# Norm gains in the splits of the transposed tiles, another order of the first loads, and part of the high parts on POOL

## The chip, the core and the metric

The kernel runs on one core of a Trainium2 chip. The core has five engines that run side by side, each through its own list of instructions in order: TensorE (PE in the profile; PEld is its loading of weights), VectorE (DVE), ScalarE (ACT), GpSimd (POOL), and SyncE (SP), which here issues nearly all DMA transfers. They wait for each other by semaphores. Matmuls read SBUF and write PSUM. The metric is the device time of one execution in microseconds (us), the median of several.

## What is computed

Two layers of an encoder on 512 tokens of width 1024. Each layer has a mixer (12 token heads of self-attention in 3 key/value groups, and 4 heads of attention to a memory of 256 rows) and a gated feed-forward block, each with a norm before and after it. What matters here is how the norms before the products go into them:

```python
def rms_norm(x, g):
    xf = x.astype(jnp.float32)
    y = xf * lax.rsqrt(jnp.mean(xf * xf, axis=-1, keepdims=True) + EPS)
    return (y * g.astype(jnp.float32)).astype(x.dtype)
...
    mem_n = rms_norm(mem, mem_norm_g)
    for i in range(DEPTH):
        h = rms_norm(x, g_mix_pre[i])
        proj = h @ w_in[i]                  # queries, keys, values, memory queries
        ...
        mkv = mem_n @ w_mem_kv[i]           # memory keys and values
```

The gain g scales the 1024 columns of x or mem, and so the rows of the weight that multiplies them: it may be applied to either side of the product. The row factor (rsqrt) is applied to the product's rows, behind the matmul.

## The kernel before

**Products in three parts.** Products run in fp32r, a format that keeps part of fp32. Each fp32 operand is split into a high part (hi, a copy rounded to fp32r) and a low part (lo = operand - hi), and each product is three matmuls: hi by hi, hi by lo, lo by hi (`mm3`, L275 to L279). `split` (L281) makes the two parts: hi on ACT or, with bit 2 of its argument set, on POOL; lo on DVE or, with bit 1 set, on POOL. `split_scaled` (L298) does the same and multiplies by a factor of one value per partition; its lo is always DVE's.

**Layer 0's mixer.** x and mem come already transposed from HBM (`xT`, `memT`: 128 channels by 8 chunks by 128 tokens). `start` (L1152) issues the first loads and splits token tile 0 into hT (hi and lo), then the key/value weights `wkv` in four units of 768 columns, with token tile 1 after the second unit; `parts(t)` splits a token tile in two instructions of 128x512 per part, `mem_parts(m)` a memory tile in one of 128x1024. Token tiles 2 and 3, memory tiles 0 and 1 and the row factors of x (`factors`: two sums of squares on ACT, then three small operations on POOL, and a fourth for the queries) come later, at due times in the table `LATE`.

Then PE computes keys and values for four token tiles from hT and `wkv` (24 matmuls a tile, in pieces of two channel chunks; tiles 0 and 1 interleaved), the first half of the memory keys and values from mT and `wm` units 0 and 1 (24 matmuls), query group 0 from hT and `wq`, and with it the second half of the memory product, then the other query groups among the heads. `again` (L416) copies the keys' high part on POOL into a third section that the transposes at L430 read. `normalise` (L616) scales the softmax rows p on POOL before they are transposed at L636.

**Weights.** `unit` (L212) loads a weight unit into one of three raw buffers (`raw`, L265) and splits it into one of four pairs whi and wlo. In layer 0 it gets the norm's gain as `g`: where `side` is even it uses `split_scaled`; where it is odd (lo on POOL) it first scales the raw weight in place on POOL (L243) and then splits it. The sides stand in the table `PACE`: for layer 0, `wkv` 0, 0, 2, 0; `wm` 2, 1, 1, 0; `wq` 1, 0, 0, 1 for groups 0 and 1, and 3 for all units of groups 2 and 3.

**What sets the order.** PE's order is the program's order, which `mixer` (L676) writes by sorting pieces by due time. On the other engines the scheduler orders instructions by readiness and program order when the program is built; once built, each engine runs its list in order. The first loads are chained on SP (`queued`, L1200), each after the one before; `self.after` (L188, L223) keeps the first weights of `unit` behind the memory's loads.

Of the kernel before, what the change touches and what calls it, by code (L numbers as in the profile page):

```python
# [16 lines left out]
P = 128  # L17
# [168 lines left out]
class Trunk:  # L186
    def __init__(self, tc, a):
        self.tc, self.nc, self.a, self.nraw, self.more, self.after = tc, tc.nc, a, 0, None, None  # L188
        self.pairs, self.todo, self.stores = {}, [], []
# [22 lines left out]
    def unit(self, src, side=0, pool=None, parts=1, put=None, x=0, dst=None, key=None, g=None, raw=None, pair=None):  # L212
# [3 lines left out]
        own = raw  # L216
# [9 lines left out]
        def load():  # L226
            raw = own or self.raw()
            hi, lo = [(pool or self.whl).tile([P, 1024], F32R, tag=z, name=f"w{z}", bufs=4) for z in ("hi", "lo")]
            if not own:
                with self.tc.issue_after(self.after) if self.after else nullcontext():  # L230
                    nc.sync.dma_start(raw[:, :n], src)
            return raw, hi, lo
# [150 lines left out]
    def mem_pieces(self, l, mk, put, x0, dx, lag, xw):  # L383
# [3 lines left out]
        for u in range(4):  # L387
            self.unit(self.a["wm"][l, u], self.side(l, "mw", u), put=put, x=xw[u], dst=w, key=u,
                      g=self.gcol[:, 1, 2 * u:2 * u + 2])
# [119 lines left out]
    def q_pieces(self, l, c, qTs, put, x0, lead):  # L509
        nc = self.nc  # L510
        w = {}
        for z in range(2):
            self.unit(self.a["wq"][l, c, z], self.side(l, "qw", 2 * c + z), put=put, x=x0 - lead + z * lead / 3, dst=w,
                      key=z, g=None if l else self.gcol[:, 0, 4 * z:4 * z + 4], pair=("wq", l, c, z))
# [161 lines left out]
    def mixer(self, l, mkp, late, tokp):  # L676
# [53 lines left out]
        if l == 0:  # L730
            put(0, lambda: setattr(self, "after", None))
# [420 lines left out]
    def start(self, mkp):  # L1152
# [3 lines left out]
        with ExitStack() as st:  # L1156
# [24 lines left out]
            def parts(t):  # L1181
                for q in range(2):
                    c = slice(t * P, t * P + P)
                    self.split(self.hT[0][q][:, :, c], self.hT[1][q][:, :, c], xT[t][:, 4 * q:4 * q + 4])

            def mem_parts(m):
                c = slice(m * P, m * P + P)
                self.split(self.mT[:, 0, :, c], self.mT[:, 1, :, c], mT[m])

            parts(0)  # L1190
            self.wkv = []
            for u in range(4):
                self.wkv.append(self.unit(a["wkv"][0, u], side=self.side(0, "kw", u), g=gcol[:, 0, 2 * u:2 * u + 2],
                                          raw=raw[u]))
                if u == 1:
                    parts(1)
# [16 lines left out]

        def loads():
            turn(2)
            row(0)
            row(1)
            turn(3)
            row(2)
            for m in range(2):  # L1220
                mT.append(turned("memT"))
                queued(mT[m], a["memT"][m])
            self.after = last[-1]
            row(3)

# [126 lines left out]
```

## Time and profile before

| | us |
|---|---|
| median of 3 runs (1119.73 to 1121.31) | 1120.67 |
| the profiled execution, whole | 1120.98 |
| its span, first to last instruction | 1119.2 |
| PE busy in the span | 1092.2 |
| DVE busy | 835.4 |
| ACT busy | 660.9 |
| POOL busy | 203.3 |

The profiled execution is 0.3 us above the median; some 1.8 us of it lie outside the span. The views used below are these. The page has busy times, and the costliest groups of instructions: line, engine, operation, tiles as out<-in, shape, count, then busy us, mean ns of one, idle us of the engine before them and what ended it. The waits list who waited for whom: us in total, times, longest. The timeline has start, length, engine, line, operation, tiles, shape, count, and in brackets the idle time before and who ended it. Windows give, for a stretch, its length, the busy us and count of PE, PEld, DVE, ACT and POOL, the granted TensorE clock, the DMA share and GB/s. PE's busy time counts a matmul's whole length, of which neighbours overlap a part.

### The profile page before, as it was taken

To read this page: it belongs to the slowest core of one execution; us is meant where nothing else is said; L and a number is where in the kernel's file an instruction comes from. 1 tells how busy PE (TensorE), PEld (TensorE's weight loads), DVE (VectorE), ACT (ScalarE), POOL (GpSimd) and SP (SyncE) were. 2 spreads that over 40 slices of the span, in tenths; PEclk is the share of its full clock that TensorE was granted. 3 is DMA by queue.
4 is the path that set the end of the run, shared out by engine and by line. 5 is a ranking of instruction groups with operands and counts; after the bars stand their busy time and mean duration, and the time that the engine had idled before them with its cause. 6 is when DMAs were issued, how large, how long until landed. Compare 5 with 4: busy or idle time off the path is not lost.

```text
span 1119.2 us, 19475 instructions
## 1 busy us (share of the span) xinstructions
PE 1092.2 (98%) x7438; PEld 1002.9 (90%) x7438; DVE 835.4 (75%) x1399; ACT 660.9 (59%) x1347; POOL 203.3 (18%) x349
## 2 busy tenths in 40 slices
PE   8989999999999999999999999999999999999997
PEld 6879988899989989998899888878999899899986
DVE  5568886899656867885797988757996478669855
ACT  7568995665435544553566888756665255345631
POOL 3685331201100000000343553312000000000001
PEclk9899999999999999999999999999999999999999
DMA  8521115533752382326453221145136223413253
GB/s 331 213 71 39 39 38 189 189 119 120 254 198 79 111 288 87 97 95 206 147 193 114 76 76 38 39 149 183 47 114 210 73 76 114 150 58 99 89 169 113
DMA packets 40558, 142.43 MB, mean 127 GB/s; under 512 B 4625, under 2 KB 5009, under 8 KB 40337
## 3 DMA queue, kind: packets, MB, share of 16 engines
q1 hardware_dynamic: 40176, 140.66, 37.3%
q8 instruction: 58, 0.95, 0.4%
q10 hardware_dynamic: 288, 0.53, 0.1%
q14 instruction: 36, 0.29, 0.1%
HBM read 122.30 MB, written 18.87 MB: 126 GB/s over the span
## 4 chain that ended last, share of the span: by engine, by line
PE 82%; DVE 5%; POOL 5%; ACT 4%; issue 2%; DMA 2%; DVEq 0%; POOLq 0%; SPq 0%; ACTq 0%
PE ps L278 12%; PE ps L277 12%; PE ps L279 12%; PE ps L1036 12%; PE ps L1034 12%; PE ps L1035 12%; PE tp L636 3%; PE o L651 2%; PE o L650 2%; PE s L575 1%; PE s L576 1%; POOL raw L243 1%; POOL wlo L289 1%; DVE tl L291 1%; POOL r L311 1%
## 5 line engine op out<-in xcount | busy, mean ns | idle before, releaser
L287 ACT ACTIVATE whi<-raw 128x1024 fp32r<-128x1024 f32 (+2 forms) x186 | 158.5, 863 | 178.4 <-PE ps L1036 73.5
L291 DVE TENSOR_TENSOR wlo<-raw,whi 128x1024 fp32r<-128x1024 f32 (+2 forms) x178 | 175.3, 995 | 72.4 <-ACT whi L287 69.7
L1035 PE MATMUL ps<-sf,wlo 128*128 128x256 f32 x640 | 179.7, 281 | 0.0
L1034 PE MATMUL ps<-sf,whi 128*128 128x256 f32 x640 | 179.7, 281 | 0.0
L1036 PE MATMUL ps<-sf,whi 128*128 128x256 f32 x640 | 179.7, 281 | 0.0
L277 PE MATMUL ps<-whi,f 128*128 128x512 f32 (+1 forms) x360 | 138.6, 385 | 0.0
L278 PE MATMUL ps<-wlo,f 128*128 128x512 f32 (+1 forms) x360 | 138.5, 385 | 0.0
L279 PE MATMUL ps<-whi,f 128*128 128x512 f32 (+1 forms) x360 | 138.4, 384 | 0.0
L1036 PE MATMUL ps<-a,whi 128*128 128x256 f32 x480 | 134.4, 280 | 0.0
L1034 PE MATMUL ps<-a,whi 128*128 128x256 f32 x480 | 134.3, 280 | 0.0
L1035 PE MATMUL ps<-a,wlo 128*128 128x256 f32 x480 | 133.8, 279 | 0.0
L1035 PEld LDWEIGHTS ps<-sf,wlo 128*128 128x128 f32 x640 | 121.4, 190 | 0.5
L1034 PEld LDWEIGHTS ps<-sf,whi 128*128 128x128 f32 x640 | 121.1, 189 | 0.5
L1036 PEld LDWEIGHTS ps<-sf,whi 128*128 128x128 f32 x640 | 121.4, 190 | 0.0
L320 POOL TENSOR_SCALAR e<-sso 128x1 f32<-128x1 f32 x8 | 3.4, 420 | 563.8 <-ACT junk L315 563.6
L277 PE MATMUL ps<-whi,hT 128*128 128x256 f32 (+1 forms) x320 | 99.0, 309 | 0.8 <-ACT whi L304 0.8
L278 PE MATMUL ps<-wlo,hT 128*128 128x256 f32 (+1 forms) x320 | 94.4, 295 | 1.8 <-DVE wlo L291 1.3
L626 POOL TENSOR_SCALAR p<-p,rd 128x256 f32<-128x256 f32 (+2 forms) x128 | 76.5, 616 | 101.3 <-DVE rd L623 42.0
L279 PE MATMUL ps<-whi,hT 128*128 128x256 f32 (+1 forms) x320 | 93.9, 293 | 0.0
L1035 PEld LDWEIGHTS ps<-a,wlo 128*128 128x128 f32 x480 | 90.5, 188 | 0.2
L1034 PEld LDWEIGHTS ps<-a,whi 128*128 128x128 f32 x480 | 90.5, 188 | 0.2
L1036 PEld LDWEIGHTS ps<-a,whi 128*128 128x128 f32 x480 | 90.1, 188 | 0.0
(205 smaller groups left out, 2729.5 us busy)
## 6 DMA issues: line engine op xcount, KB each, us to landing
raw<-in_wgu_dram SPq DMA_DIRECT2D x48, 512.0 KB, 4.4
raw<-in_wd_dram SPq DMA_DIRECT2D x44, 512.0 KB, 4.3
rb<-in_wgu_dram SPq DMA_DIRECT2D x40, 512.0 KB, 3.6
raw<-in_wo_dram SPq DMA_DIRECT2D x17, 512.0 KB, 3.6
raw<-in_wq_dram SPq DMA_DIRECT2D x16, 512.0 KB, 5.5
xt<-x SPq DMA_DIRECT2D x12, 512.0 KB, 5.0
raw<-in_wm_dram SPq DMA_DIRECT2D x8, 512.0 KB, 3.7
x<-y SPq DMA_DIRECT2D x8, 512.0 KB, 3.0
```

Of the source, the lines that this page charges most:

```text
L277: mm(out, lh, rh, start=first, stop=False)
L278: mm(out, lh, rl, start=False, stop=False)
L279: mm(out, ll, rh, start=False, stop=last)
L287: a = nc.scalar.activation(hi, src, AF.Copy)
L291: b = nc.vector.tensor_sub(lo, src, hi.bitcast(F32))
L626: self.pooled = nc.gpsimd.tensor_scalar(hd["p"][z][:, :n], hd["p"][z][:, :n], rd[:, z:z + 1], 1.0, op0=OP.mult, op1=OP.mult)
L636: nc.tensor.transpose(tp[:, z], hd["p"][i][:, jj * P:(jj + 1) * P], self.ident)
L650: nc.tensor.matmul(o[:, c0:c1], hd["v"](j), th, start=(j == 0), stop=False, skip_group_check=True)
L651: nc.tensor.matmul(o[:, c0:c1], hd["v"](j), tl, start=False, stop=last, skip_group_check=True)
L1034: mm(out, wh[:, s], rh, start=start and k == 0, stop=False, skip_group_check=True)
L1035: mm(out, wl[:, s], rh, start=False, stop=False, skip_group_check=True)
L1036: mm(out, wh[:, s], rl, start=False, stop=k == 3, skip_group_check=True)
```

## The change

The gain moves from the weights to the other operand. `parts` and `mem_parts` now call `split_scaled` chunk by chunk (128x128, eight for a tile) with the gain of that chunk, and weights are split without a gain. For token tiles 1 to 3 and both memory tiles the high parts of the odd chunks are made on POOL. Since no unit has `g` any more, the in-place scaling on POOL does not occur, and a `wkv` unit is split whole (unit 0 in two halves). Of token tile 0 the first four chunks are split ahead of `wkv` unit 0, the last four behind it, and tile 1 behind unit 1.

The first loads are chained in another order: `wm` unit 0 goes ahead of the second row tile, memory tile 0 behind the last token tile, `wm` unit 1 ahead of memory tile 1, and the first `wq` unit behind the last row tile. They fill three raw buffers early (`early`), and `self.after` is gone.

```diff
-    def unit(self, src, side=0, ..., g=None, raw=None, pair=None):
+    def unit(self, src, side=0, ..., g=None, raw=None, pair=None, early=None):
-        own = raw
+        own = raw or self.early.pop(early, None)
...
-                with self.tc.issue_after(self.after) if self.after else nullcontext():
-                    nc.sync.dma_start(raw[:, :n], src)
+                nc.sync.dma_start(raw[:, :n], src)
...
             self.unit(self.a["wm"][l, u], self.side(l, "mw", u), put=put, x=xw[u], dst=w, key=u,
-                      g=self.gcol[:, 1, 2 * u:2 * u + 2])
+                      early=("wm", u) if l == 0 else None)
...
-                      key=z, g=None if l else self.gcol[:, 0, 4 * z:4 * z + 4], pair=("wq", l, c, z))
+                      key=z, pair=("wq", l, c, z), early=("wq", z) if l == c == 0 else None)
...
-            def parts(t):
-                for q in range(2):
-                    c = slice(t * P, t * P + P)
-                    self.split(self.hT[0][q][:, :, c], self.hT[1][q][:, :, c], xT[t][:, 4 * q:4 * q + 4])
+            def parts(t, qs=range(2)):
+                c = slice(t * P, t * P + P)
+                for k in range(4 * qs[0], 4 * qs[-1] + 4):
+                    self.split_scaled(self.hT[0][k // 4][:, k % 4, c], self.hT[1][k // 4][:, k % 4, c], xT[t][:, k],
+                                      gcol[:, 0, k:k + 1], 2 * (t > 0 and k % 2))
             def mem_parts(m):
                 c = slice(m * P, m * P + P)
-                self.split(self.mT[:, 0, :, c], self.mT[:, 1, :, c], mT[m])
-            parts(0)
+                for k in range(KD):
+                    self.split_scaled(self.mT[:, 0, k, c], self.mT[:, 1, k, c], mT[m][:, k], gcol[:, 1, k:k + 1],
+                                      2 * (k % 2))
+            parts(0, (0,))
             self.wkv = []
             for u in range(4):
-                self.wkv.append(self.unit(a["wkv"][0, u], side=self.side(0, "kw", u), g=gcol[:, 0, 2 * u:2 * u + 2],
-                                          raw=raw[u]))
-                if u == 1:
-                    parts(1)
+                self.wkv.append(self.unit(a["wkv"][0, u], side=self.side(0, "kw", u), raw=raw[u], parts=1 if u else 2))
+                if u < 2:
+                    parts(*((0, (1,)), (1,))[u])
...
         def loads():
             turn(2)
             row(0)
+            raw("wm", 0, a["wm"][0, 0])
             row(1)
             turn(3)
+            mem_turn(0)
             row(2)
-            for m in range(2):
-                mT.append(turned("memT"))
-                queued(mT[m], a["memT"][m])
-            self.after = last[-1]
+            raw("wm", 1, a["wm"][0, 1])
+            mem_turn(1)
             row(3)
+            raw("wq", 0, a["wq"][0, 0, 0])
```

PE's list is the same before and after. Three places on DVE and POOL show how the others moved; each row is a line, an operation, tiles as out<-in, a shape and how often it stands there in a row. The changed kernel's lines are one lower up to L680 or so (L290 is the subtraction of `split`, L304 that of `split_scaled`).

DVE's first instructions, from the first low parts of token tile 0 on, before:

```order
L291 TENSOR_TENSOR hT<-xT,hT 128x4x128 x2
L305 SCALAR_TENSOR_TENSOR wlo<-raw,cst,whi 128x384 x4
L291 TENSOR_TENSOR hT<-xT,hT 128x4x128 x2
L305 SCALAR_TENSOR_TENSOR wlo<-raw,cst,whi 128x384 x4
L291 TENSOR_TENSOR hT<-xT,hT 128x4x128 x2
```

and now:

```order
L304 SCALAR_TENSOR_TENSOR hT<-xT,cst,hT 128x128 x4
L290 TENSOR_TENSOR wlo<-raw,whi 128x384 x2
L304 SCALAR_TENSOR_TENSOR hT<-xT,cst,hT 128x128 x6
L290 TENSOR_TENSOR wlo<-raw,whi 128x768
L304 SCALAR_TENSOR_TENSOR hT<-xT,cst,hT 128x128 x6
L290 TENSOR_TENSOR wlo<-raw,whi 128x768 x2
L304 SCALAR_TENSOR_TENSOR hT<-xT,cst,hT 128x128 x8
```

The low part of `wkv` unit 1 stood right behind that of unit 0; now six parts stand between them, the last two of them of token tile 1 (its chunks 1 and 3, whose high parts are POOL's).

POOL from a row factor of x (e, rs, rs, rq) to the first weights of the memory and query products, before (k are the keys that `again` copies):

```order
L320 TENSOR_SCALAR e<-ss 128x1
L325 TENSOR_TENSOR rs<-e,ss 128x1
L326 TENSOR_TENSOR rs<-rs,mhalf 128x1
L1234 TENSOR_SCALAR rq<-rs 128x1
L302 TENSOR_SCALAR whi<-raw,cst 128x512 x2
L418 TENSOR_SCALAR k_484<-k_484 128x3x64
L243 TENSOR_SCALAR raw<-raw,cst 128x512 x2
L289 TENSOR_TENSOR wlo<-raw,whi 128x512
L243 TENSOR_SCALAR raw<-raw,cst 128x256
L289 TENSOR_TENSOR wlo<-raw,whi 128x512
L243 TENSOR_SCALAR raw<-raw,cst 128x256 x3
L289 TENSOR_TENSOR wlo<-raw,whi 128x512 x2
```

and now:

```order
L284 TENSOR_SCALAR whi<-raw 128x512 x2
L417 TENSOR_SCALAR k_375<-k_375 128x3x64
L301 TENSOR_SCALAR mT<-memT,cst 128x128 x3
L319 TENSOR_SCALAR e<-ss 128x1
L324 TENSOR_TENSOR rs<-e,ss 128x1
L325 TENSOR_TENSOR rs<-rs,mhalf 128x1
L1243 TENSOR_SCALAR rq<-rs 128x1
L288 TENSOR_TENSOR wlo<-raw,whi 128x512 x2
L301 TENSOR_SCALAR mT<-memT,cst 128x128
L417 TENSOR_SCALAR k_445<-k_445 128x3x64
L301 TENSOR_SCALAR mT<-memT,cst 128x128 x3
```

The first memory weight (whi) stood behind the row factor of the last token tile; now it stands two row factors earlier, that of tile 2 behind it and that of tile 3 behind the second memory weight (wlo) and the second memory tile. The row factor of tile 3 and the wlo of the first query weight follow.

POOL around the two copies of the memory keys (k, 128x4x64), before:

```order
L243 TENSOR_SCALAR raw<-raw,cst 128x256 x2
L418 TENSOR_SCALAR k_766<-k_766 128x4x64
L243 TENSOR_SCALAR raw<-raw,cst 128x256 x5
L285 TENSOR_SCALAR whi<-raw 128x512 x2
L418 TENSOR_SCALAR k_791<-k_791 128x4x64
L289 TENSOR_TENSOR wlo<-raw,whi 128x512 x2
L243 TENSOR_SCALAR raw<-raw,cst 128x256 x5
L626 TENSOR_SCALAR p<-p,rd 128x256
```

and now:

```order
L284 TENSOR_SCALAR whi<-raw 128x512 x2
L417 TENSOR_SCALAR k_816<-k_816 128x4x64
L288 TENSOR_TENSOR wlo<-raw,whi 128x512 x2
L284 TENSOR_SCALAR whi<-raw 128x512 x2
L417 TENSOR_SCALAR k_841<-k_841 128x4x64
L288 TENSOR_TENSOR wlo<-raw,whi 128x512 x2
L625 TENSOR_SCALAR p<-p,rd 128x256
```

The scaling of raw weights is gone, and the split of one query unit of group 2 (two wlo and, for the next unit, two whi) has moved between the two copies.

More of the change, by code (lines that the diff above doesn't have):

```diff
@@ L187, in __init__ @@
     def __init__(self, tc, a):
-        self.tc, self.nc, self.a, self.nraw, self.more, self.after = tc, tc.nc, a, 0, None, None
+        self.tc, self.nc, self.a, self.nraw, self.more, self.early = tc, tc.nc, a, 0, None, {}
         self.pairs, self.todo, self.stores = {}, [], []
@@ L210, in ahead, with unit @@
             self.stores = [(self.pairs[(name, *at)][z], pair[z].bitcast(F32)) for z in range(2)]
-    def unit(self, src, side=0, pool=None, parts=1, put=None, x=0, dst=None, key=None, g=None, raw=None, pair=None):
+    def unit(self, src, side=0, pool=None, parts=1, put=None, x=0, dst=None, key=None, g=None, raw=None, pair=None, early=None):
         nc, n = self.nc, src.shape[-1]
-        own = raw
+        own = raw or self.early.pop(early, None)
         if pair in self.pairs:
@@ L730, in mixer @@
         if l == 0:
-            put(0, lambda: setattr(self, "after", None))
             put(-0.5, lambda: nc.gpsimd.tensor_scalar(self.nsink, self.sink, -1.0, 1.0, op0=OP.mult, op1=OP.mult))
@@ L1212, in turn, with mem_turn, raw @@
                 queued(xT[t][:, 4 * z:4 * z + 4], a["xT"][t, z])
+        def mem_turn(m):
+            mT.append(turned("memT"))
+            queued(mT[m], a["memT"][m])
+        def raw(name, u, src):
+            self.early[name, u] = self.raw()
+            queued(self.early[name, u], src)
         def loads():
```

## The prediction

> **What bounds the kernel now.** I read the page's busy times first, then the waits of PE over the first 130 us, then PE's timeline where those waits lie, then windows over the same stretch.
>
> ```profile
> PE 1092.2 (98%) x7438; PEld 1002.9 (90%) x7438; DVE 835.4 (75%) x1399; ACT 660.9 (59%) x1347; POOL 203.3 (18%) x349
> PE ps L277 <- POOL whi L302: 4.0, 1, 4.0
> PE tp L430 <- POOL k L418: 3.0, 2, 2.1
> PE tp L636 <- POOL p L626: 1.6, 2, 1.4
> PE ps L278 <- DVE wlo L305: 1.3, 2, 1.0
> ```
>
> TensorE is busy for 98% of the span, its order of instructions is written by hand, and the change leaves that order alone. So time can come only from PE's gaps and from stretches at a low clock. Of the 27 us without a matmul (1119.2 - 1092.2) these four waits hold 9.9, all before 80 us; the first three are for POOL, an engine with 18% load. The change touches layer 0's mixer only, so the rest of the span should run as before. The first gap:
>
> ```profile
> 24.38 0.34 PE L279 MATMUL ps<-whi,hT 128*128 128x384 f32 x1
> 28.72 0.80 PE L277 MATMUL ps<-whi,mT 128*128 128x512 f32 x1 [4.01 <-POOL whi L302]
> 39.59 0.35 PE L277 MATMUL ps<-whi,hT 128*128 128x256 f32 x1
> ```
>
> The key/value products (hT) end at 24.7; the memory products (mT) start at 28.7; the row at 39.59 stands among the first query products. The later gaps, and POOL beside them:
>
> ```profile
> 65.70 0.54 PE L430 MATMUL tp<-identr,k 128*128 128x128 f32 x4 [0.86 <-POOL k L418]
> 69.67 0.54 PE L430 MATMUL tp<-identr,k 128*128 128x128 f32 x4 [2.11 <-POOL k L418]
> 75.12 0.33 PE L636 MATMUL tp<-cst,p 128*128 128x128 f32 x1 [1.40 <-POOL p L626]
> 75.68 0.43 PE L636 MATMUL tp<-cst,p 128*128 128x128 f32 x1 [0.23 <-POOL p L626]
> 65.62 2.46 POOL L243 TENSOR_SCALAR raw<-raw,cst 128x256 f32<-128x256 f32 x5
> 69.22 0.40 POOL L418 TENSOR_SCALAR k<-k 128x256 fp32r<-128x256 f32 x1
> ```
>
> PE stands still for a copy that takes POOL 0.40 us, because POOL first scales raw weights. Then the clock, in windows of 3.41 us laid from where it fell:
>
> ```profile
> 27.92:31.33 3.41, 1.57 (x3) 0.97 (x4) 3.08 (x7) 0.94 (x3) 2.37 (x5) 0.51 0.03 10
> 31.33:34.74 3.41, 3.41 (x10) 2.63 (x9) 0.21 (x1) 1.26 (x2) 3.33 (x5) 0.50 0.67 237
> 65.46:68.87 3.41, 1.86 (x16) 1.72 (x16) 2.09 (x6) 3.06 (x9) 3.41 (x8) 1.00 0.43 149
> 72.29:75.70 3.41, 1.78 (x12) 1.27 (x12) 2.87 (x11) 2.21 (x6) 3.41 (x8) 1.00 0.47 154
> 75.70:79.11 3.41, 3.41 (x17) 3.41 (x18) 1.01 (x4) 1.59 (x5) 0.94 (x2) 0.51 0.00 0
> ```
>
> After the length come the busy times of PE, PEld, DVE, ACT and POOL, then the granted clock. Behind a window with PE busy 1.78 us the clock was 0.51 for one window; behind one with 1.86 it stayed.
>
> **Part 1: POOL no longer scales raw weights (L243).**
>
> ```profile
> L243 POOL TENSOR_SCALAR raw<-raw,cst 128x256 f32<-128x256 f32 x24 | 11.3, 484 | 7.1 <-DMA raw<-in_wq_dram 7.1
> L243 POOL TENSOR_SCALAR raw<-raw,cst 128x512 f32<-128x512 f32 x4 | 3.4, 860 | 0.1
> L289 POOL TENSOR_TENSOR wlo<-raw,whi 128x512 fp32r<-128x512 f32 x15 | 19.6, 1318 | 0.2
> L285 POOL TENSOR_SCALAR whi<-raw 128x512 fp32r<-128x512 f32 x8 | 5.0, 636 | 0.1
> 56.66 0.40 PE L279 MATMUL ps<-whi,mT 128*128 128x512 f32 x1
> ```
>
> All 28 instructions go, 14.7 us of POOL's time. Between the two memory-key copies (k, x4) stand now two whi and two wlo: 2 x 0.64 + 2 x 1.32 = 3.9 us. The product that the first copy needs ends at 57.0 on PE; with 1.5 for its two parts on ACT and DVE the copy ends near 59, the second near 63.5. Without the waits PE wants the second at 69.67 - 2.11 - 0.86 = 66.7. The two wlo behind it end near 66.2, before the first p, which PE wants at 75.12 - 1.40 - 2.97 = 70.8. So all four waits go: 0.86 + 2.11 + 1.40 + 0.23 = 4.6 us. The window at 0.51 goes with them: it lost between nothing and 3.41 x 0.49 = 1.7; I take 1.5, since nearly all of it was matmuls. **Part 1: -6.1 us.** Late next is p's chain on DVE and ACT (minimum, exp, reciprocal), by my sum about 1 us ahead of PE.
>
> **Part 2: the start.**
>
> ```profile
> 4.40 0.31 ACT L1197 ACTIVATE identr<-cst 128x128 fp32r<-128x128 f32 x1 [1.47 <-DMA cst<-in_cst_dram]
> 4.62 0.61 ACT L287 ACTIVATE hT<-xT 128x512 fp32r<-128x512 f32 x1
> 38.90 1.70 ACT L304 ACTIVATE whi<-raw,cst 128x256 fp32r<-128x256 f32 x4
> 52.41 1.67 DVE L305 SCALAR_TENSOR_TENSOR wlo<-raw,cst,whi 128x256 fp32r<-128x256 f32 x4 [0.68 <-ACT whi L304]
> L291 DVE TENSOR_TENSOR hT<-xT,hT 128x512 fp32r<-128x512 f32 x8 | 5.2, 687 | 4.2 <-ACT hT L287 4.1
> 18.10 0.19 POOL L1234 TENSOR_SCALAR rq<-rs 128x1 f32<-128x1 f32 x1
> 8.31 0.34 PE L277 MATMUL ps<-whi,hT 128*128 128x384 f32 x1
> 20.29 0.41 PE L277 MATMUL ps<-whi,hT 128*128 128x384 f32 x1
> ```
>
> A split of 128x512 becomes four scaled ones of 128x128, a form that the trace does not show. On ACT it costs between 0.22 (4.40 to 4.62, the unscaled copy of that shape) and 1.70 / 4 = 0.42 (scaled, twice the columns): I take 0.30. On DVE, between 0.19 (a 128x1 operation, on POOL) and 1.67 / 4 = 0.42: 0.26. On POOL, between 0.19 and 0.48: 0.35, the middle. Scaled or not, weights cost nearly the same per column, so that their gain goes is worth nothing in itself.
>
> ACT does four splits from 4.62, wkv0's whi in two halves to 6.8, four splits to 8.0, and wkv1's whi whole (768 columns, 0.85) to 8.8. PE begins with wkv0 as before, but its next product (before: 8.31, its second matmul 0.17 later) waits for wkv1's wlo. That stands on DVE behind four parts of tile 0 and the two of tile 1 whose hi is POOL's, and takes 0.95 (0.69 for 512 columns). Undisturbed it ends at 9.8. But DVE and POOL hold each other up:
>
> ```profile
> 57.72 1.29 POOL L289 TENSOR_TENSOR wlo<-raw,whi 128x512 fp32r<-128x512 f32 x1
> 57.86 1.24 DVE L444 TENSOR_TENSOR qx<-qx,rt 128x64 f32<-128x64 f32 x1
> ```
>
> DVE's 64 columns ended 0.09 after POOL's wlo, a microsecond late. Strict turns between the engines would put wlo's end at 11.2; I take 10.2, because POOL's pieces are small here. [...]
>
> PE's second matmul of that product then starts at 10.3 (bounds 9.9 and 11.3) against 8.5: **+1.8 us**. Between 7.43 and 10.85, the window of the same raster, PE is busy about 1.7 of 3.41 us, less than the 1.78 that cost the clock, so I expect one window near half clock: **+1.7**. The first product of token tile 3 (before: 20.29 + 1.1 = 21.4) then ends at T = 24.9; bounds 22.8 and 25.9.
>
> T matters because the first memory weight's buffers are wkv0's, and that product reads them last. The loads are no limit:
>
> ```profile
> 13.70 0.96 SPq L1202 DMA_DIRECT2D memT<-in_memT_dram  x2
> memT<-in_memT_dram SPq DMA_DIRECT2D x2, 512.0 KB, 6.2
> ```
>
> The second memT lands at 14.7 + 6.2 = 20.9 now; two weights of 512 KB pass it in SP's queue, 1.3 us each at some 0.4 MB/us, which makes 23.5. Row and xT loads behind the first move by 1.3, and their users wait on PE by then. From T, a chain with POOL in it leads to query group 0: POOL, two whi 1.3, a copy 0.35, three mT parts 1.05 and 0.3 of DVE's turns, three small operations (row factor) 1.0: T + 4.0. ACT, keys, values and half of wm1's whi, 1.4: T + 5.4. POOL, two wlo 2.6, four mT parts and a copy 1.75, three small 1.0: T + 10.7. ACT again 1.4; POOL, two wlo 2.6: T + 14.7. PE's six matmuls 0.7: **T + 15.4**. From T + 4.5 to about T + 9 PE has little to do, for the second memory tile's parts stand behind those wlo: the first gap is moved and cut up, not removed. Before, the same six matmuls ended at 39.59 + 0.7 = 40.3. **Part 2: T + 15.4 - 40.3 = 0.0**, bounds -2.1 and +1.0 by T, and 1.5 either way for the chain.
>
> **Sum.** The profiled execution took 1120.98 (span 1119.2), 0.3 above the median of the runs: 1120.98 - 6.1 + 0.0 = 1114.9; less 0.3: **1114.6 us**.
>
> **Rivals.** *The clock holds at the start.* A half-busy window may pass, as that with 1.86 did; then T is 23.2, part 2 gives -1.7 and the time is 1112.9. For it: 1.7 is an estimate, 0.1 under the dividing rows. [...]
>
> *The late stage has another bound.*
>
> ```profile
> 110.00:120.00 10.00, 9.77 (x77) 9.36 (x77) 9.82 (x31) 9.70 (x29) 3.85 (x7) 1.00 0.17 54
> ```
>
> DVE and ACT are nearly full once all heads run, and may be what p waits for when POOL is free. Part 1 then gives 1.2: 1120.98 - 1.2 - 0.3 = 1119.5. Against it: the waits named POOL.
>
> [...]
>
> **How the numbers follow.** Forecast 0.43, clock holds 0.35, another bound 0.15, one port 0.07. The range runs from part 2 at -2.1 - 1.5 (1111.0, with 0.2 more from part 1: 1110.8) to +1.0 + 1.5 with part 1 at -5 (1118.2); I give 1110.5 to 1118.3, which holds some four fifths. A measurement here tells 0.2% (2.2 us) from no change: faster 0.83 (the first two and a third of the third), same 0.10, slower 0.07.
>
> **What would show it.** Right: no wait of PE for k's copy or p before 80 us, and clock 1.00 there; a wait of PE for wkv1's wlo near 9 us with a window near 0.5 behind it; waits of PE for mT between T + 4 and T + 9. Wrong: PE idle at the transposes of k or p; that wlo after 11.3; the query products' six matmuls ending after 42.

## The result, and the profile after

| | before | changed |
|---|---|---|
| median of the runs, us | 1120.1 (7 runs, 1119.69 to 1121.6) | 1117.86 (7 runs, 1116.35 to 1118.46) |
| ratio to before, with its 95% interval | | 0.9974 (0.9963 to 0.9986) |
| the profiled execution, us | 1120.98 | 1118.46 |
| its span, us | 1119.2 | 1116.6 |

The changed kernel is faster by 2.2 us, or 0.26%; 6.1 were forecast. 1117.86 lies in the range of the prediction (1110.5 to 1118.3), near its upper end. The page of the changed kernel, busy times:

```profile
PE 1091.1 (98%) x7438; PEld 1002.4 (90%) x7438; DVE 842.1 (75%) x1430; ACT 660.1 (59%) x1359; POOL 196.7 (18%) x340
```

The waits of PE over the first 130 us (who waited for whom, us in total, times, longest):

```profile
PE ps L276 <- ACT mT L303: 4.5, 1, 4.5
PE ps L276 <- ACT whi L286: 1.3, 2, 0.8
PE tp L429 <- DVE kmb L430: 1.3, 1, 1.3
...
PE ps L277 <- DVE wlo L290: 1.2, 2, 1.0
PE ps L278 <- DVE mT L304: 0.7, 1, 0.7
```

The three waits for POOL are gone. The long gap has moved from the first memory tile to the second, and one new wait stands at the copy of the memory keys' second part (kmb). PE's timeline at these places:

```profile
8.95 0.44 PE L276 MATMUL ps<-whi,hT 128*128 128x384 f32 x1 [0.58 <-ACT whi L286]
10.40 0.45 PE L277 MATMUL ps<-wlo,hT 128*128 128x384 f32 x1 [1.01 <-DVE wlo L290]
...
23.84 0.41 PE L276 MATMUL ps<-whi,hT 128*128 128x384 f32 x1
...
34.14 0.50 PE L276 MATMUL ps<-whi,mT 128*128 128x512 f32 x1 [4.48 <-ACT mT L303]
...
35.53 0.80 PE L278 MATMUL ps<-whi,mT 128*128 128x512 f32 x1 [0.65 <-DVE mT L304]
...
41.80 0.35 PE L276 MATMUL ps<-whi,hT 128*128 128x256 f32 x1
...
69.29 0.51 PE L429 MATMUL tp<-identr,k 128*128 128x128 f32 x4 [1.30 <-DVE kmb L430]
```

The row at 23.84 opens the first product of token tile 3, the row at 41.80 the six matmuls of query group 0 that the prediction timed (at 39.59 before). The clock, in windows that begin where the trace of this execution changes it (length, then busy PE, PEld, DVE, ACT, POOL, clock, DMA share, GB/s):

```profile
7.64:11.05 3.41, 1.82 (x10) 1.26 (x9) 3.41 (x9) 3.11 (x8) 3.16 (x5) 1.00 0.97 367
11.05:14.47 3.42, 3.42 (x12) 3.42 (x11) 3.42 (x7) 1.33 (x5) 2.43 (x6) 0.50 0.75 272
28.12:31.53 3.41, 1.54 (x7) 0.86 (x5) 2.44 (x10) 1.31 (x4) 2.01 (x7) 1.00 0.72 238
31.53:34.95 3.42, 0.73 (x2) 0.30 (x2) 3.42 (x6) 1.97 (x7) 3.40 (x5) 1.00 0.58 225
34.95:38.36 3.41, 2.83 (x7) 2.25 (x8) 3.19 (x12) 2.30 (x8) 2.34 (x7) 0.50 0.45 154
65.67:69.08 3.41, 2.33 (x23) 2.15 (x21) 3.40 (x8) 2.12 (x5) 3.41 (x4) 1.00 0.49 154
```

Two windows run at half clock at the start, behind PE's two gaps; the late one of before (75.70) is gone.

**Where the time went.** PE's list is the same in both kernels, so the start of each matmul in one trace can be set against the start of the same matmul in the other. The difference, changed less before, at some places (times of before):

```
matmul at, us            8.49   21.25  40.25  42.4   65.70  69.67  75.12  81.9   300    500    640    last
changed less before, us +1.91  +3.55  +2.22  +2.06  +0.49  -0.38  -1.96  -4.00  -4.18  -3.73  -2.73  -2.59
```

Three stretches come out of it. The start costs 2.06 us up to 42 us (part 2; forecast 0.0). From 42 to 82 us PE gains 6.06 (part 1; forecast 6.1). Behind 82 us it gives 1.4 back (from -4.00 to -2.59), where the forecast has nothing. 1119.2 + 2.06 - 6.06 + 1.4 = 1116.6, the span.

### The profile page after: what moved, and what is told of

It is laid out like the page before. It is cut to its first block, busy times and chain, and to the rows that moved or that the text cites. A ratio compares the mean times of both kernels' runs of the same rounds, so it can differ in the third digit from the quotient of the medians.

```text
span 1116.6 us, 19512 instructions
## 1 busy us (share of the span) xinstructions
PE 1091.1 (98%) x7438; PEld 1002.4 (90%) x7438; DVE 842.1 (75%) x1430; ACT 660.1 (59%) x1359; POOL 196.7 (18%) x340
## 4 chain that ended last, share of the span: by engine, by line
PE 87%; DVE 6%; ACT 3%; POOL 2%; issue 1%; DMA 1%; DVEq 0%; POOLq 0%; ACTq 0%
PE ps L277 14%; PE ps L278 14%; PE ps L276 14%; PE ps L1034 12%; PE ps L1032 12%; PE ps L1033 12%; PE tp L635 3%; PE o L650 2%; PE o L649 2%; PE s L574 1%; PE s L575 1%; DVE tl L290 1%; DVE wlo L290 1%; DMA pair<-whi 1%; POOL r L310 1%
## 5 line engine op out<-in xcount | busy, mean ns | idle before, releaser
L286 ACT ACTIVATE whi<-raw 128x512 fp32r<-128x512 f32 (+3 forms) x204 | 168.7, 843 | 175.5 <-PE ps L1034 73.7
L290 DVE TENSOR_TENSOR wlo<-raw,whi 128x1024 fp32r<-128x1024 f32 (+3 forms) x199 | 192.5, 980 | 75.7 <-ACT whi L286 72.0
```

What stands on the lines that cost most here:

```text
L286: a = nc.scalar.activation(hi, src, AF.Copy)
L290: b = nc.vector.tensor_sub(lo, src, hi.bitcast(F32))
```

## Experiments

Three theories were on trial. For the start: the new pieces on POOL and DVE stretch the chain (A), or windows at half clock that were not priced do (B), or the order of loads or the chain through POOL's weights does (C). For the late part: the gain comes from the scalings alone. For what is given back: chance, or a fixed effect.

In the table, T is the end of token tile 3's first product (its last matmul's end; the prediction's T, one pitch earlier, is 0.2 less). "Tile 2" is the start of the first product with the second memory tile and "six" the end of the six query matmuls, both from T. The next three columns are PE against before, by the same matmul as above, products of zeros left out; then the windows at half clock before 45 us. The ratio, with its interval, is to the runs of before on the same chip in the same session (medians 1119.9 to 1120.7). Median and ratio come from 5 to 11 runs, every other column from one profiled execution. The rows "changed" and "e11_after_again" are the same kernel, so what they differ by is the execution's: 1.1 us in T, 1.6 in "six".

| run | median us | ratio (95%) | T | tile 2 | six | at 42 us | 42 to 82 | behind 82 | half clock |
|---|---|---|---|---|---|---|---|---|---|
| before | 1120.1 | | 21.6 | 11.3 | 18.9 | | | | 2 |
| changed | 1117.86 | 0.9974 (0.9963 to 0.9986) | 25.1 | 9.0 | 17.6 | +2.06 | -6.1 | +1.4 | 2 |
| e1_late_gain | 1116.36 | 0.9960 (0.9948 to 0.9973) | 24.0 | 9.8 | 17.8 | +1.34 | -5.9 | -0.1 | 2 |
| e2_old_loads | 1116.68 | 0.9969 (0.9957 to 0.9981) | 23.9 | 10.8 | 17.8 | +0.98 | -6.0 | -0.1 | 2 |
| e3_all_act | 1115.44 | 0.9953 (0.9940 to 0.9965) | 24.2 | 8.7 | 16.5 | 0.00 | -5.8 | +0.1 | 1 |
| e4_warm_both | 1116.05 | 0.9957 (0.9944 to 0.9969) | 23.9 | 9.0 | 17.9 | +1.10 | -5.9 | -0.1 | 1 |
| e5_q_dve | 1119.89 | 0.9998 (0.9989 to 1.0006) | 23.7 | 9.0 | 18.5 | +1.49 | -1.3 | -0.3 | 2 |
| e6_m_dve | 1117.00 | 0.9969 (0.9957 to 0.9981) | 24.9 | 7.2 | 17.2 | +1.45 | -5.8 | +0.3 | 3 |
| e7_more_pool | 1120.82 | 1.0006 (0.9997 to 1.0014) | 24.1 | 13.2 | 22.3 | +5.78 | -6.0 | +0.1 | 3 |
| e8_act_warm | 1116.07 | 0.9960 (0.9948 to 0.9973) | 24.3 | 10.0 | 16.3 | -0.07 | -5.9 | +1.0 | 0 |
| e9_whole_parts | 1116.45 | 0.9966 (0.9954 to 0.9978) | 22.7 | 10.0 | 18.1 | +0.07 | -5.8 | +0.6 | 1 |
| e10_mem_act | 1117.24 | 0.9969 (0.9958 to 0.9980) | 25.1 | 8.8 | 16.8 | +1.13 | -5.8 | +1.0 | 2 |
| e11_after_again | 1118.43 | 0.9981 (0.9973 to 0.9990) | 24.0 | 9.0 | 19.2 | +2.49 | -6.0 | +1.2 | 2 |
| e12_act_warm20 | 1114.69 | 0.9949 (0.9934 to 0.9963) | 24.1 | 8.7 | 15.0 | -1.59 | -6.0 | +1.3 | 0 |

**The late gain alone.** The kernel before, with this edit:

```diff
-                      key=z, g=None if l else self.gcol[:, 0, 4 * z:4 * z + 4], pair=("wq", l, c, z))
+                      key=z, g=None if l or c else self.gcol[:, 0, 4 * z:4 * z + 4], pair=("wq", l, c, z))
```

> The kernel before, with the norm gain left out of the query weights of groups 1 to 3 (so their in-place scalings on POOL, 20 of the 28, are gone; the queries of these groups lack the gain). Start and loads are as before. Theory (the late waits and the slow window came from those scalings alone): TensorE stands at the same place up to 55 us and is 6.0 us early at 82 us, the time is 1114.1 us; if part of that is given back behind 400 us as in the changed kernel (there 1.3 us), 1115.4. Rival (the late gain needed the changed start, which puts all splits earlier): at most 3 us early at 82 us, 1117 or more.

From 42 to 82 us PE gains 5.9 us, with the start of before: the scalings alone carry part 1. At 82 us it is only 4.5 early, since this execution's start was 1.3 us later; the median, 1116.36, is above the theory's 1114.1. ACT's timeline:

```profile
6.95 1.12 ACT L304 ACTIVATE whi<-raw,cst 128x384 fp32r<-128x384 f32 x2 [0.66 <-DMA raw<-in_wkv_dram]
```

The first weight landed a microsecond later than in the profile of before (whi there at 5.93), and a window at half clock followed. The engines' lists up to 42 us are those of before, so the edit itself does not touch the start. But all five runs (1115.16 to 1116.68) lie above the 1114.5 that 5.9 us off 1120.44 would give, so it is not shown that the late start is one execution's chance; why it came stays open.

**The old order of loads.** The changed kernel with the loads of before (and `self.after` back, to hold `unit`'s loads behind the memory's):

```diff
             row(0)
-            raw("wm", 0, a["wm"][0, 0])
             row(1)
             turn(3)
-            mem_turn(0)
             row(2)
-            raw("wm", 1, a["wm"][0, 1])
-            mem_turn(1)
+            for m in range(2):
+                mem_turn(m)
+            self.after = last[-1]
             row(3)
-            raw("wq", 0, a["wq"][0, 0, 0])
```

> The changed kernel with the first loads in the order of before. Theory (the loads are no limit; TensorE and the chain of splits set the start): within 1.2 us of the changed kernel, 1116.7 to 1119.1, and the first product of token tile 3 ends at 24.9 us as there. Rival (the new order is what lets the first memory weight be split in time): the first memory product starts 1 us or more later than 28.1 us, the time is 1119.5 or more.

Time and T are those of the theory, within what the clock's windows make. The rival's first half came true too, and cost nothing in the end; PE's timeline:

```profile
30.80 0.79 PE L277 MATMUL ps<-whi,mT 128*128 128x512 f32 x1 [3.82 <-POOL whi L285]
```

With the old order PE waits 3.8 us ahead of the first memory tile and none ahead of the second; with the new order 4.5 ahead of the second. The six end 17.8 after T here, and 17.6 and 19.2 in the two profiles of the changed kernel. The order of the loads decides where the gap lies; that the new one shortens it is not shown.

**All high parts on ACT.**

```diff
-                                      gcol[:, 0, k:k + 1], 2 * (t > 0 and k % 2))
+                                      gcol[:, 0, k:k + 1], 0)
...
-                                      2 * (k % 2))
+                                      0)
```

> The changed kernel with all high parts of the transposed tiles on ACT, none on POOL. Theory (POOL and DVE hold each other up, and that stretched the chain to the row factors by 1.3 us): the row factor behind the first memory weight comes 1 us or more earlier than 30.2 us, TensorE's wait of 4.5 us for the second memory tile shrinks to 3.5 or less, the time is 1115.5 to 1117. Rival (ACT has no room for 20 more parts of 0.39 us at a spacing of 0.30): waits for ACT grow at the start, 1118.5 to 1120.

The row factor is ready at 27.8 instead of 30.2, PE's wait is 2.6, and the time is 1115.44, as the theory had it within 0.1 us. The shorter wait is mostly PE's own lateness, though: PE now waits 1.0 us behind T for DVE's low parts of token tiles and starts the first memory product at T + 4.5 instead of T + 3.0. The second memory tile itself comes 0.3 earlier, at T + 8.7, and its low part, for which PE waited 0.65 us in the changed kernel, is there in time.

```profile
32.91 0.80 PE L276 MATMUL ps<-whi,mT 128*128 128x512 f32 x1 [2.61 <-ACT mT L303]
```

**Zeros in the gaps.** Ahead of the two waiting products stand small bf16 matmuls of a zero tile, which add nothing to an open sum:

```diff
+    def warm(self, out, n):
+        for _ in range(n):
+            self.nc.tensor.matmul(out[:, :256], self.zero[:, :P], self.zero, start=False, stop=False)
...
+            if l == 0 and (u, m) == (0, 1):
+                self.warm(ps[0], 28)
...
+            if l == 0 and (t, u) == (0, 1):
+                self.warm(ps, 8)
```

> The changed kernel with small products of zeros added to open sums in TensorE's two gaps of the start: 8 ahead of the product with the second key/value unit, 28 ahead of the first product with the second memory tile. Theory (two windows at half clock cost some 1.5 us each, and behind the second the chain through POOL takes over, its weight ending at 41.3 us): granted clock 1.00 in both windows, TensorE 1.5 us earlier from 15 us on, 1.5 to 1.9 us earlier at 45 us, time 1116.0 to 1116.4. Rival A (the whole of both windows comes back): 1114.8. Rival B (the chain through POOL alone sets the time of the query products, TensorE's clock is covered): no more than 0.4 us, 1117.5.

The first window kept its clock and T came 1.3 us earlier. That this is the zeros' work is not shown, since the second profile of the changed kernel (below) has a T of 24.0 without them. The second fell again. The windows behind it:

```profile
31.42:34.83 3.41, 1.31 (x5) 0.78 (x5) 3.41 (x7) 2.65 (x9) 3.41 (x7) 1.00 0.52 173
34.83:38.25 3.42, 3.42 (x9) 2.65 (x8) 2.50 (x11) 2.31 (x8) 2.07 (x6) 0.50 0.23 90
```

The 28 zeros ended at 31.45, 1.4 us ahead of the tile, and their work lies in the window before. So 1116.05 is the expected time for half of the expected reason at most, and the second window stayed open.

**One query weight's low part on DVE.** In layer 0's `PACE`:

```diff
-'qw': [1, 0, 0, 1, 3, 3, 3, 3]
+'qw': [1, 0, 0, 1, 3, 2, 3, 3]
```

> The changed kernel with the low part of one query unit (second unit of group 2) on DVE instead of POOL: the two wlo of 1.3 us that stand on POOL behind the second memory-key copy. Theory (these two hold DVE's small operations to 1.2 us each, and that is why the copy kmb on DVE, for which TensorE still waits 1.3 us, is late): the wait for kmb falls to 0.3 us or less, TensorE gains 7.0 us between 55 and 82 us against 6.0 in the changed kernel, the time is 1116.8. Rival (kmb is late for its place in DVE's list, behind the masked maxima; two wlo of 0.69 us more on DVE make it later): the wait stays at 1.3 us or grows, 1117.9 or more.

PE's waits from 42 to 82 us, and DVE's timeline:

```profile
PE s L574 <- DVE vm L407: 2.6, 1, 2.6
PE tp L429 <- DVE kmb L430: 0.5, 1, 0.5
```

```profile
64.99 1.89 DVE L290 TENSOR_TENSOR wlo<-raw,whi 128x512 fp32r<-128x512 f32 x2 [4.26 <-POOL whi L284]
66.80 0.47 DVE L407 SCALAR_TENSOR_TENSOR k<-ps,rs,k 128x256 fp32r<-128x256 f32 x1
67.19 0.47 DVE L407 SCALAR_TENSOR_TENSOR vm<-ps,rs,vm 128x256 fp32r<-128x256 f32 x1
```

The wait for kmb did shrink, to 0.5, but the copy did not come sooner: it ended at 71.10 (69.15 in the changed kernel), and PE, which was held elsewhere, came late to it. What the edit does show is that POOL's work stretches DVE's small operations: the four ahead of the copy (rt, qx, qx and q) took 0.21, 0.23, 0.22 and 0.43 us with POOL idle, and 0.63, 0.54, 0.55 and 1.29 in the changed kernel beside POOL's wlo and whi (where POOL is idle, from 49.89 us on, the changed kernel's trace has 0.21, 0.22, 0.22 and 0.43 for the same four forms). DVE's list now has these two ahead of the memory keys' and values' low parts, which PE wants first; DVE stands idle 4.3 us for POOL's whi, PE waits 2.6 for vm, and windows at half clock follow. The edit lost 4.7 of the 6.0 us, and the time is on the rival's side: here the place of two instructions in a list weighed more than what they take.

**The second memory weight's low part on DVE.** In layer 0's `PACE`:

```diff
-'mw': [2, 1, 1, 0]
+'mw': [2, 0, 1, 0]
```

> The changed kernel with the low part of the second memory weight on DVE instead of POOL (two subtractions of 128x512). Theory (POOL's two wlo hold DVE's key rotation, ACT's key copy waits for that and ACT's parts of the second memory tile for the copy): the second memory tile's first product starts 1.5 us or more earlier after token tile 3's first product than the 9.2 us of the changed kernel, and the query products' six matmuls end 1.0 us or more earlier than 17.6 us after it; time 1116.9 or less. Rival (DVE is full there, 3.4 of 3.4 us): not earlier than 9.0 us, time 1117.9 or more.

The second memory tile starts 1.8 us earlier after T, as the theory says, but the six end only 0.4 earlier. Most of the difference is a wait: DVE, which now makes the weight's low part, has the tile's low part late, so that PE waits 1.25 us for it (0.65 in the changed kernel) and starts that matmul at T + 9.7 instead of T + 10.4. The rest lies in the windows:

```profile
27.92:31.33 3.41, 1.48 (x7) 0.81 (x5) 2.41 (x9) 1.35 (x4) 3.07 (x10) 1.00 0.73 222
31.33:34.74 3.41, 1.40 (x3) 0.68 (x4) 3.41 (x11) 3.08 (x10) 1.99 (x4) 0.50 0.91 311
```

Here two windows at half clock follow one another behind the gap, one more than in the changed kernel's first profile. The time, 1117.00, lies between the two lines and settles neither theory.

**Twice the parts on POOL.** 40 instead of 20:

```diff
-                                      gcol[:, 0, k:k + 1], 2 * (t > 0 and k % 2))
+                                      gcol[:, 0, k:k + 1], 2 * (t > 0))
...
-                                      2 * (k % 2))
+                                      2)
```

> The changed kernel with all high parts of token tiles 1 to 3 and of both memory tiles on POOL, 40 instead of 20. Theory (POOL's parts and DVE's run one after the other, so each part on POOL costs the chain some 0.4 us): the query products' six matmuls end 2 us or more later than 42.5 us, time 1119.9 or more. Rival (POOL's parts lie beside other work; what stretched the chain is something else): within 0.8 us of the changed kernel.

```profile
PE ps L276 <- POOL mT L301: 6.9, 1, 6.9
```

The six end at 46.5 instead of 42.75, and the time is that of before. From 0 to 20 parts the six move 1.1 us after T, from 20 to 40 another 4.7, of which 4.2 are the later second memory tile (T + 9.0 and T + 13.2); behind it three windows at half clock, not one, take their part. The first 20 parts are partly hidden, the next are not. Both of the theory's lines are reached (46.5 for 44.5, 1120.82 for 1119.9), but that POOL's parts and DVE's run one after the other is not shown: 20 more parts at 0.4 us are 8 us of POOL's own time, and PE waits for POOL itself, so the run does not tell a hold of one engine by the other from POOL's load.

**All on ACT, and zeros.** The third and fourth edits together, with

```diff
-                self.warm(ps[0], 28)
+                self.warm(ps[0], 38)
```

> All high parts of the transposed tiles on ACT as in the third experiment, with products of zeros in TensorE's two gaps, 8 in the first and 38 (28 before) in the second. Theory (with the second gap filled to its end no window falls to half clock): granted clock 1.00 up to 80 us, 1.4 us less than the third experiment's 1115.4: 1114.0. Rival (behind the second gap the chain through POOL takes the window's place): clock 1.00, but 0.5 us or less, 1114.9.

```profile
30.23 4.32 PE L282 MATMUL ps<-zero 128*128 128x256 bf16 x38
```

The clock stayed at 1.00, but with the parts on ACT the gap is 2.6 us and the zeros took 4.3: they pushed the memory tile from T + 8.7 to T + 10.0 and gave back what the clock brought. From there to the six's end PE took 6.3 us, against 7.8 in the third experiment with its slow window. The time, 1116.07, missed both lines (1114.0 and 1114.9); 1.0 us of it was given back behind 82 us.

**Unscaled, in whole pieces.**

```diff
-                for k in range(4 * qs[0], 4 * qs[-1] + 4):
-                    self.split_scaled(...)
+                for q in qs:
+                    self.split(self.hT[0][q][:, :, c], self.hT[1][q][:, :, c], xT[t][:, 4 * q:4 * q + 4])
...
-                for k in range(KD):
-                    self.split_scaled(...)
+                self.split(self.mT[:, 0, :, c], self.mT[:, 1, :, c], mT[m])
```

> The changed kernel with token and memory tiles split as before, unscaled and in pieces of 128x512 and 128x1024, so that the norm gain of layer 0 is left out altogether. Loads, weights and TensorE's order are those of the changed kernel. Theory (the pieces of 128x128 and their share on POOL are the whole cost of the start): the product with the second key/value unit waits less than 0.4 us for its low part, the query products' six matmuls end 16 us or less after token tile 3's first product, and TensorE stands 2.0 to 3.5 us earlier than before at 42 us; time 1110.8 to 1112.2. Rival (the chain through POOL's weights and row factors sets the start with or without pieces): less than 1 us earlier than before at 42 us, 1113.5 or more.

The theory fell; the rival's two lines came true. T is 2.5 us earlier than in the changed kernel's first profile, which had a slow window there, and 1.3 earlier than in its second, which had none: the second figure is nearer to what the pieces cost the first stretch. But the second memory tile comes 10.0 after T with no piece at all:

```profile
32.67 0.80 PE L276 MATMUL ps<-whi,mT 128*128 128x512 f32 x1 [4.53 <-ACT mT L286]
```

So a gap of 4.5 us stands there with none of POOL's parts. (Some of it is the whole piece, which takes ACT 1.04 us where the changed kernel's first part takes 0.39.) All told the pieces and a slow window cost 2.0 us (0.07 against 2.06 at 42 us); the medians of this kernel and of the changed one in the same session, 1116.45 and 1118.43, differ by 2.0 as well.

**Only the memory tiles' high parts on ACT.** In `mem_parts`:

```diff
-                                      2 * (k % 2))
+                                      0)
```

> The changed kernel with the high parts of the memory tiles alone on ACT; those of the token tiles stay shared with POOL. Theory (of POOL's 20 parts the eight of the memory tiles are those that stretch the chain, since they stand ahead of a row factor): the query products' six matmuls end 16.5 us or less after token tile 3's first product (17.6 in the changed kernel, 16.5 with all parts on ACT), time 1115.4 to 1116.4. Rival (the token tiles' parts are what counts): 17.4 us or more, 1117.4 or more.

The six end at T + 16.8, between the two lines and nearer to the theory's: by one profile each, eight of POOL's twenty parts make up 0.9 of the 1.1 us. The time lies between the lines too; T has its slow window here and 1.0 us is given back near 612 us.

**The changed kernel again.** No edit.

> The changed kernel again, for a second profile of it. Theory (its spread of 2.1 us comes from where the windows of the clock fall and from a race of POOL and DVE near 612 us): the clock's windows lie otherwise against the program than in the first profile, and the TensorE waits near 612 us are 0.5 or 1.0 us; the part from 42 to 82 us is 6.0 us again, whatever the other two do. Rival (each is a fixed effect of the change): a window at half clock from 11.1 us, and 1.0 us of waits for p near 612 us, again.

```profile
6.46:9.87 3.41, 2.27 (x10) 1.20 (x7) 3.20 (x9) 3.41 (x11) 1.93 (x4) 1.00 1.03 401
...
30.35:33.77 3.42, 0.73 (x2) 0.30 (x2) 3.42 (x6) 1.96 (x6) 3.34 (x5) 1.00 0.63 254
33.77:37.18 3.41, 2.77 (x8) 2.19 (x8) 3.19 (x12) 2.32 (x8) 2.40 (x8) 0.50 0.53 154
37.18:40.60 3.42, 3.42 (x10) 2.65 (x9) 2.72 (x4) 2.07 (x5) 3.08 (x3) 0.50 0.01 2
```

The same kernel, the same waits, other windows: the wait of 1.0 us near 10 us is cut in two by a boundary at 9.87, the clock holds and T is 1.1 us earlier; the gap at 30 us falls so that two windows follow it at half clock, not one. Part 1 is 6.0 again. Near 612 us the waits for p are 1.1 us again, as the rival has it.

**All on ACT, with 20 zeros.** The eighth experiment's kernel with

```diff
-                self.warm(ps[0], 38)
+                self.warm(ps[0], 20)
```

> As the eighth experiment, all high parts on ACT and products of zeros in TensorE's two gaps, but 20 instead of 38 in the second, so that they end before the gap does (20 x 0.12 = 2.4 us in a gap of 2.6). Theory (from the second memory tile on, TensorE itself needs 6.3 us to the end of the query products' six matmuls when its clock is full, and nothing else is later): the memory tile starts 8.7 us and the six end 15.0 to 15.3 us after token tile 3's first product, no window at half clock up to 80 us, TensorE 7.2 us earlier than before at 82 us, time 1114.0 if the race near 612 us goes well and 1115.1 if not. Rival (the chain through POOL's weights and row factors stands behind it, as the eighth experiment's 16.3 may mean): the six end 16 us or later, 6.0 us at 82 us, time 1115.2 to 1116.2.

```profile
29.99 2.36 PE L282 MATMUL ps<-zero 128*128 128x256 bf16 x20
32.73 0.50 PE L276 MATMUL ps<-whi,mT 128*128 128x512 f32 x1 [0.39 <-ACT mT L307]
```

```profile
27.76:31.17 3.41, 3.41 (x23) 2.85 (x22) 3.18 (x8) 2.63 (x8) 2.78 (x3) 1.00 0.96 306
31.17:34.58 3.41, 3.02 (x19) 2.27 (x18) 3.07 (x11) 3.41 (x11) 0.64 (x3) 1.00 0.85 298
```

The theory held: tile 2 at T + 8.7, the six at T + 15.0, no window at half clock, PE 7.5 us early at 82 us; 1.3 is given back behind it. 1114.69 us is the fastest of the kernels here, 3 us below the changed kernel.

## Why the prediction came out as it did

**What bounds the kernel** was right: PE's order did not change, and nearly all that was gained or lost is PE's gaps and windows at half clock.

**Part 1 was right in size: -6.06 against -6.1.** All runs but the one that moved a low part to DVE give 5.8 to 6.1, with the start of before as well. Its composition was partly wrong. The waits of 0.86, 1.40 and 0.23 went, and the slow window gave 1.6 for the 1.5 forecast. Of the wait of 2.11, though, 1.30 came back for kmb: "late next is p's chain" named the wrong work. The trace of before already had it, in DVE's timeline:

```profile
66.38 0.68 DVE L431 CAST kmb<-tp 128x512 fp32r<-128x512 f32 x1
```

PE's second transposes wait for this copy out of tp, and it ended at 67.06, behind the 66.7 at which the prediction has PE start them. In thirteen of the fourteen profiles it starts 6.4 to 6.7 us behind the same matmul of PE (the one at 59.97 before), so it did not move up with POOL's scalings gone. What sets its place is not shown: POOL's work stretches DVE's operations ahead of it, but the one edit meant to test that (the fifth experiment) made it later. What made up for it are a wait of 0.3 for qT, which the waits of before list and the prediction left out, and that PE lost 0.18 us beyond its idle time: between the matmuls of 69.67 and 75.12 it gained 1.58 us for a wait of 1.40.

**Part 2: T was right, 24.94 for 24.9, partly by luck.** The product with the second key/value unit got its low part 1.91 us late (forecast 1.8) and the window behind it cost 1.64 (forecast 1.7). The first of these stands in every run with the pieces (1.3 to 2.1 at that matmul; 1.0 without them in the ninth experiment). The second was the luck of one execution: the prediction laid the windows on the raster of the trace of before, and the eleventh experiment shows the same wait with the clock kept. Of the eight profiles with the pieces and without zeros, three have a slow window there.

**Part 2: the step that failed is "T + 15.4".** It came as T + 17.6. The prediction let the chain through POOL end last and put nothing beside it; in the trace PE's own work behind the gap ended last, slowed by a window at half clock that the sum did not have, and the chain was late as well. POOL from the changed kernel's T on:

```profile
25.23 1.49 POOL L284 TENSOR_SCALAR whi<-raw 128x512 fp32r<-128x512 f32 x2 [0.92 <-PE ps L278]
26.70 0.78 POOL L417 TENSOR_SCALAR k<-k 128x192 fp32r<-128x192 f32 x1
27.46 1.55 POOL L301 TENSOR_SCALAR mT<-memT,cst 128x128 fp32r<-128x128 f32 x3
...
29.64 0.55 POOL L325 TENSOR_TENSOR rs<-rs,mhalf 128x1 f32<-128x1 f32 x1
...
31.55 2.64 POOL L288 TENSOR_TENSOR wlo<-raw,whi 128x512 fp32r<-128x512 f32 x2 [1.08 <-ACT whi L286]
...
36.72 0.55 POOL L325 TENSOR_TENSOR rs<-rs,mhalf 128x1 f32<-128x1 f32 x1
...
38.63 2.66 POOL L288 TENSOR_TENSOR wlo<-raw,whi 128x512 fp32r<-128x512 f32 x2 [1.01 <-ACT whi L286]
```

- The chain. The row factor of tile 2 is ready at 30.19, T + 5.25 for T + 4.0: whi 1.49 for 1.3, the copy 0.78 for 0.35, three parts 1.55 for 1.05 with 0.3 of turns, the small ones and the start the rest. The second leg lost 0.35 more (37.27, T + 12.3 for 10.7), and the weight of the query product ended at 41.29, T + 16.35 for 14.7. PE did not wait for it: behind the wait of 0.65 at 35.53 PE has no gap up to 42.75, and the six's first product with that weight starts at 41.99. So the chain, though late, did not set the six; with the clock at full speed it would have held them to some T + 17 (an estimate: 41.29 and the 0.76 from 41.99 to 42.75).
- PE behind the gap. The prediction said that PE has little to do from T + 4.5 to T + 9 (it waited 4.48 us until T + 9.2), and put no slow window behind it, though it had priced one behind a shorter wait at the start. From the second memory tile to the end of the six PE took 8.6 us: 6.4 of work at full clock (as in the twelfth experiment), the wait of 0.65 for the tile's low part, and 1.6 for the window.

Taking the parts off POOL (third experiment) ended the chain 3.1 us sooner after T, but the six only 1.1, from 17.6 to 16.5: 0.3 by the second tile, 0.65 by the wait for its low part, the rest in the window. With the parts on ACT, taking the window away as well brings the six from T + 16.5 to T + 15.0, a little below the forecast.

So the forecast's T + 15.4 is what this kernel does when neither of the two is there. The window alone was not taken away with the parts still on POOL: the fourth experiment tried, and it fell again.

**"The rest of the span should run as before" was wrong by 1.4 us.** Most of it (0.95) is one place in layer 1's heads. POOL's and DVE's timelines of the third experiment's kernel, where nothing is given back, and of the changed kernel, at the same instructions:

```profile
610.55 1.60 POOL L625 TENSOR_SCALAR p<-p,rd 128x512 f32<-128x512 f32 x2
611.75 0.67 DVE L457 TENSOR_TENSOR rt<-qx,gt 128x256 f32<-128x256 f32 x1
```

```profile
612.85 1.86 POOL L625 TENSOR_SCALAR p<-p,rd 128x512 f32<-128x512 f32 x2
613.82 0.41 DVE L457 TENSOR_TENSOR rt<-qx,gt 128x256 f32<-128x256 f32 x1
```

Either POOL's p comes first and DVE's product takes 0.67, or DVE's comes first in 0.41 and p is 0.26 later; PE waits for p, and the delay grows to 1.0 us in the next heads. Of the fourteen profiles nine have 0.5 or 0.6 us of waits for p there and five have 1.0 or 1.1, both profiles of the changed kernel among the five. No single edit separates the two groups, and what tips the race was not found. The other 0.4 us, lost at two matmuls near 400 us, has no wait listed against it and stays open.

**The rivals.** "Another bound" is out (part 1 is about 6 in every kernel but the fifth experiment's, where an edit took it). The slowdown, which has 0.07 in the list of chances, did not come with 20 parts on POOL (1117.86); with 40 the whole gain went (1120.82), for a cause that is not told apart. "The clock holds at the start" was a matter of the execution, and did hold in the second profile; it did not give 1112.9, since behind it stand the same chain and two slow windows. The lines that were to show the prediction wrong did their work: "the six matmuls ending after 42" is what happened (42.5), and it points at the step that failed.

## What to carry to other kernels

Where an engine of low load is waited for, taking small jobs from it can bring the whole wait, up to what is late next (here 4.6 us of waits for POOL went, and 1.30 came back behind DVE's kmb): read that from the trace too. Jobs that such an engine is given cost nothing only while the chain to the next wait has slack; here the six ended 1.1 us later with 20 small parts on POOL and 5.9 with 40, slow windows included. Price a gap of TensorE with the window at half clock behind it, some 1.6 us in these traces, as a chance that the execution draws (the same kernel had one and two of them behind the same gap), unless the gap can be filled with harmless matmuls that end just before the awaited operand comes (20 of them in the twelfth experiment, clock 1.00 behind them). Before work is moved to another engine to mend one late instruction, read that engine's list at that place: the fifth experiment lost 4.7 us there.

## What was not expected of the hardware

- The windows of the clock are not tied to the program. In these traces they are 3.41 us long (the changed kernel's clock falls at 11.05 and is back at 14.46, and the falls of one trace lie whole windows apart: 27.98 and 75.77 before, 11.05 and 34.95 in the changed kernel), and their boundaries lie otherwise in each execution: the first fall came at 27.98 (before), 11.05 and 33.77 (the changed kernel, twice), 8.39 (the first experiment) or 29.48 us (the second). The two profiles of the changed kernel have one program, and 11.05 and 33.77 are 6.66 windows apart, so the raster of before, on which the prediction laid its windows, could not place them.
- PE's busy time did not tell which window costs the clock. At full clock, windows with 1.54 (the changed kernel), 1.57 (its second profile) and 1.82 us busy (the tenth experiment) were kept and windows with 1.48 (the sixth), 1.78 (before) and 1.82 us (the changed kernel) were not; in the traces of before and of the changed kernel none with 1.86 or more fell. At half clock, a window with 2.77 us busy (the changed kernel's second profile) was followed by another at half clock and one with 2.83 (its first) was not.
- Beside a POOL subtraction of two SBUF operands, two DVE instructions with two SBUF operands lasted to its end. DVE and ACT of the changed kernel beside the two wlo of 31.55:

```profile
31.39 0.20 DVE L442 TENSOR_TENSOR kx<-kx,cst 128x48 f32<-128x48 f32 x1
...
31.77 1.27 DVE L443 TENSOR_TENSOR kx<-kx,rt 128x48 f32<-128x48 f32 x1
32.96 1.38 DVE L304 SCALAR_TENSOR_TENSOR mT<-memT,cst,mT 128x128 fp32r<-128x128 f32 x1
```

```profile
33.44 0.36 ACT L286 ACTIVATE k<-kx 128x192 fp32r<-128x192 f32 x1 [1.45 <-DVE kx L443]
33.70 1.27 ACT L303 ACTIVATE mT<-memT,cst 128x128 fp32r<-128x128 f32 x4
```

A DVE addition of 48 columns took 1.27 us instead of 0.20, a part of 128x128 1.38 instead of 0.35, ACT waited 1.45 behind it, and that is the last link ahead of PE's product behind the wait of 4.48. Both DVE instructions end within 0.15 us of a POOL wlo's end. A DVE instruction that reads a score tile s, which TensorE writes to PSUM, was not held: p<-s,mask,nsink of 128x256 at 63.97 took 0.48 us beside POOL's two wlo of 62.39 to 64.93, and 0.47 with POOL idle (at 67.58 in the fifth experiment).
